# Sample stage of a hybrid decoder step: one DMA per cache page, TensorE in written order with rows of the output projection as filler, output weights loaded ahead of the pages

## The chip, the cores and the metric

The kernel runs on one NeuronCore of a Trainium2 chip. The metric is the device time of one execution in microseconds (us). Before the change three runs took 1098.09, 1099.56 and 1103.59 us; their median, 1099.56 us, is the number to beat.

## What is computed

The reference is one step of a layer with three groups of heads that all read the same projection of the normalised input: an NSA group (compressed, selected and window attention), an RWKV-7 group and a memory group. Their outputs are gated, concatenated and multiplied by one output projection `w_out`. There is a prompt of 1024 rows and a batch of 8 samples with one new row each, whose past of 1024 rows lies in 8 cache pages that a page table names. The part that matters here is what is done for the samples, and the output projection:

```python
def nsa_decode_seq(q, pt_row, rows4_new, rows_w_new, win_buf, gates, pool, ...):
    past = pool[pt_row].reshape(-1, 4, NSA_KV_HEADS, HEAD_DIM)       # 8 pages of 128 rows
    rows4 = jnp.concatenate([past, rows4_new], axis=0)
    ck, cv, cend, ksb, vsb, ov = nsa_context(rows4, ...)             # compressed keys and values
    o_c, o_s = cmp_sel_attend(q, qpos, ck, cv, cend, ksb, vsb, ov)   # compressed and selected attention
    ...

def mixer_out(o_nsa, z_nsa, o_rw, z_rw, o_mem, z_mem, w_out):
    cat = jnp.concatenate([o_nsa.reshape(b, t, NSA_W) * jax.nn.silu(z_nsa),
                           o_rw * jax.nn.silu(z_rw), o_mem.reshape(b, t, MEM_W) * jax.nn.silu(z_mem)], axis=-1)
    return cat @ w_out
```

## The kernel before

The program has three phases. `phase1` projects the input, `phase2` does the attention of the prompt with the small work of the samples between its parts, and `phase3` does the NSA attention of the samples and the output projection of everything. The change is in phase 3, and in how memory is shared out between phases 2 and 3.

A page of the cache is laid out in memory as 128 rows of 512 numbers: 256 that the compression reads (`x`) and 256 with the selected keys and values (`kv`). `pages` loads the 8 pages of one sample: SyncE (SP) reads the page's number from the table into a register and issues two DMAs of 128 KB, one for each half. `compress` then multiplies the `x` half of a sample with the weights of the compression, 16 matmuls a sample into the tiles `p_hid`, with two short chains of ScalarE (ACT) and VectorE (DVE) work behind them. After four samples `nsa_four` takes the group on: compressed keys and values (`p_co`), a norm and rotation on DVE, transposes (`p_ckT`), scores (`p_cs`), a softmax, the choice of blocks (`p_cT`, `p_imp`), the long softmax over 1025 columns (`s_sel`), transposes of it (`p_PT`), the sum over values (`p_os`) and the last transpose (`p_oT`). Each of these steps waits for the one before it, and most of them go from TensorE (PE) to DVE or ACT and back. The scores of the selected keys (`p_ss`) are made ahead of it. Sample 0's pages are loaded in phase 2.

The prompt's output projection is cut in two halves of 512 columns. `wo_half` loads 8 pieces of `w_out` (`wor`, 256 KB each, through a pool `wst` of 4 buffers) and splits each into a rounded part `woh` (ACT) and a remainder `wol` (DVE). `out_rows` does one block of 128 rows: 24 matmuls into `p_out`, after `split_cat` has split the block's input into `chi` (ACT) and `clo` (DVE); GpSimd (POOL) loads the residual `xres` and stores the sum. There are 8 blocks a half, and `out_proj_sample` does the 8 sample rows with the weights of both halves at the end.

The order in phase 3 is set by the scheduler of the tile framework, by what is ready and by the order in which the code is written: the pages of both groups are written first, half 1 (`W1`) is written ahead of the second `nsa_four`, half 0 (`W0`) behind it. A helper `InOrder` pins TensorE's instructions to the written order; phase 2 uses it with a clock that adds up the matmuls' sizes, so that generators of work can be interleaved by that clock. Phase 3 before the change uses TensorE directly.

Pools of one phase stand where pools of the phase before stood, and a tile of the new phase waits until the tiles under it have been used for the last time. `small2` and `wk` come first in phase 2, `small3`, `wk3`, `wst` and `wop` in phase 3.

Of the kernel before, what the change touches and what calls it, by code (L numbers as in the profile page):

```python
# [21 lines left out]
NS = 8  # L22
# [4 lines left out]
KB = 2  # L27
# [9 lines left out]
RATE = {i: (0.8, 0.8, 1, 1) if i > 3 else (1.5, 1.5, 1.5, 0) for i in range(8)}  # L37
START = (1.0, 0.0, 0.7, 0.0)
# [74 lines left out]
class Step:  # L113
# [846 lines left out]
    def compress(self, xt, n, hid):  # L960

        nc = self.nc
        V, A, PE = nc.vector, nc.scalar, nc.tensor
        V.memset(hid[:, :, 63:64], 0.0)
        for e in range(2):
            ps = self.pM.tile([128, n, 64], F32, name="p_hid", tag="m")
            for m in range(8):
                self.last_hid = PE.matmul(ps[:], self.w1s[e][:, m].rearrange("p a b -> p (a b)"), xt(e, m), start=(m == 0), stop=(m == 7))  # L968
            hs = self.wk.tile([64, n, 63], F32, name="c_hs", tag="c_hs")
            A.activation(hs[:], ps[64:, :, 1:], AF.Copy)  # L970
            V.tensor_tensor(hs[:], hs[:], ps[:64, :, :63], op=OP.add)
            th = self.wk.tile([64, n, 63], F32, name="c_th", tag="c_th")
# [198 lines left out]
    def q_stack(self, i):  # L1171
# [3 lines left out]
        q = self.kt.tile([128, 12, 64], F32, name="q7") if first else self.wk.tile([128, 12, 64], F32, name="q", tag="q", bufs=2)  # L1175
        nc.sync.dma_start(q[:].rearrange("p h d -> p (h d)"), self.q_d[i * 128:(i + 1) * 128, :])
        qs = self.qs[i] = (self.kt if i % 2 else self.wk).tile([128, 12, 128], F32R, name="qs", tag="qs")
        for b in (0, 1, 2):
            pool, tag, nb = (self.kt, "kd4", KB) if first else (self.wk, "qhl", 2)
# [9 lines left out]
    def load_z(self, i):  # L1189
        cat = self.cat[i] = self.slot(i, [128, 8, 128], F32, f"cat{i}")  # L1190
        y = self.y_rw[i] = self.wk.tile([128, 256], F32, name="y_rw", bufs=2)
# [3 lines left out]
    def attn_cmp(self, i):  # L1195
# [5 lines left out]
        sc = self.wk.tile([128, 4, 128], F32, name="sc", tag="sc")  # L1201
# [10 lines left out]
        pcq = self.wk.tile([128, 8, 64], F32, name="pcq", tag="pcq")  # L1212
# [131 lines left out]
    def attn_mem(self, i):  # L1344
# [5 lines left out]
        for c in range(2):  # L1350
            nm = self.small.tile([128, 2], F32, name="nm_m")
            sm = self.small.tile([128, 2], F32, name="sm_m")
            pm = self.wk.tile([128, 2, 256], F32, name="pmem", tag="pmem", bufs=2)
# [84 lines left out]
    def phase2(self):  # L1438
        tc, nc, I, O = self.tc, self.nc, self.I, self.O
        with ExitStack() as ctx:  # L1440
            P = lambda name, bufs, **k: ctx.enter_context(tc.tile_pool(name=name, bufs=bufs, reuse_waits="tile", **k))
            self.small = P("small2", 2)
            self.wk = P("wk", 1)
# [127 lines left out]
    def sample_setup(self):  # L1571
# [9 lines left out]
        qmb = self.qmb = self.wk.tile([128, 2, NS, 32], F32, name="qmb")  # L1581
# [7 lines left out]
        x, sq, xr = (self.wk.tile([128, 8, NS], F32, name=f"s_x{k}") for k in range(3))  # L1589
# [12 lines left out]
        tab = self.wk.tile([128, 7, NS], F32, name="s_tab")  # L1602
# [65 lines left out]
    def four_keys(self, name, n):  # L1668
# [6 lines left out]
        return KT + [self.wk.tile([128, 512], F32, name=name, tag="sk", bufs=3)[:] for _ in range(2)]  # L1675

    def four_pT(self, p, n):
# [5 lines left out]
        pT = self.wk.tile([128, 4, 128], F32, name="s_pT", tag="s_pT")  # L1683
# [3 lines left out]
    def sample_mem(self):  # L1687
# [15 lines left out]
        def rest(a, p):  # L1703
# [8 lines left out]
            o = self.wk.tile([128, 256], F32, name="m_o", tag="s_p")  # L1712
# [14 lines left out]
        for a in range(2):  # L1727
# [10 lines left out]
            p = self.wk.tile([128, 256], F32, name="m_p", tag="s_p")  # L1738
# [4 lines left out]
    def sample_win(self):  # L1743
# [24 lines left out]
        def rest(a, p):  # L1768
# [8 lines left out]
            o = self.wk.tile([128, 128], F32, name="w_o", tag="s_p")  # L1777
# [9 lines left out]
        for a in range(2):  # L1787
# [8 lines left out]
            p = self.wk.tile([128, 512], F32, name="w_p", tag="s_p")  # L1796
# [4 lines left out]
    def pages(self, s, x, kv):  # L1801

        nc = self.nc
        for j in range(8):
            with self.tc.issue_after(self.last_page.ins):
                n = nc.sync.value_load(self.ptab[0:1, 8 * s + j:8 * s + j + 1], min_val=0, max_val=self.I["c_pool"].shape[0] - 1)  # L1806
            page = self.I["c_pool"][bass.ds(n, 1)].rearrange("o p c -> (o p) c")
            nc.sync.dma_start(x[:, j], page[:, 0:256])  # L1808
            self.last_page = nc.sync.dma_start(kv[:, j], page[:, 256:512])  # L1809

    def nsa_ahead(self):
# [8 lines left out]
        self.pg = [self.arena(k, "pg")[:].rearrange("p (n c) -> p n c", n=8) for k in range(2)]  # L1820
# [3 lines left out]
    def sample_nsa(self):  # L1824
# [3 lines left out]
        with ExitStack() as ctx:  # L1828
# [15 lines left out]
            with P("snsx") as xp:  # L1844

                def place(name):
                    if name in ("a0", "a1"):
                        t = self.arena(int(name[1]), "pg")[:]
                    else:
                        t = fresh.pop(name, None) or xp.tile([128, 2048], F32, name="pg", tag=name)  # L1850
                        t = t[:]
                    return t.rearrange("p (n c) -> p n c", n=8)

                fresh = {}
                for name in ("x0", "x1", "v2", "v3", "v1", "v4", "v5"):
                    fresh[name] = xp.tile([128, 2048], F32, name="pg", tag=name)
                X = [None, "x0", "x1", "a0", "x0", "x1", "a0", "x0"]
                K = [None, "v1", "v2", "v3", "v4", "v5", "v1", "a1"]
                for a in range(2):
                    VS = []  # L1860
                    hid = dp.tile([128, 4, 2, 64], F32, name="shid")
                    for s in range(4 * a, 4 * a + 4):
                        if s:
                            x, kv = place(X[s]), place(K[s])
                            self.pages(s, x, kv)
                        else:
                            x, kv = self.pg
                        VS.append(kv)
                        xm = x.rearrange("p n (e g m c) -> p e m g n c", e=2, g=2, m=8)
# [4 lines left out]
                    with tc.issue_after(self.last_hid.ins):  # L1874
                        for h in range(2):
                            for k in range(4):
                                PE.matmul(pS[h][32 * k:32 * k + 32], self.qb[:, 4 * a + k, :], VS[k][:, 4 * h:4 * h + 4, 0:128],
                                          start=True, stop=True)
                    if a:
                        W1 = self.wo_half(self.wop, 1)  # L1880
                        self.out_proj_prompt(1, W1)
                    self.nsa_four(a, hid, pS, VS, vn, dp)
            W0 = self.wo_half(ctx.enter_context(P("wop2")), 0)
            self.out_proj_prompt(0, W0)
            self.out_proj_sample((W0, W1))

    def nsa_four(self, a, hid, pS, VS, vn, dp):
# [13 lines left out]
        o = self.norm_rope(ck[:].rearrange("p s d -> p (s d)")[:, None, :], 3, 1, 4, 9)  # L1901
        pk = self.pT.tile([128, 4, 128], F32, name="p_ckT", tag="t")
# [3 lines left out]
        V.tensor_copy(kt[:], pk[:64])  # L1906
        pc = self.pM.tile([128, 128], F32, name="p_cs", tag="m")
# [13 lines left out]
        V.tensor_copy(im[:], pi[:])  # L1921
        pi2 = self.pM.tile([128, 16], F32, name="p_imp2", tag="m")
# [13 lines left out]
        V.tensor_scalar(sc[:], sc[:], self.gr[:, a, 0:1], None, op0=OP.mult)  # L1936
        srcs = [sl[:, j * 128:(j + 1) * 128] for j in range(8)] + [sc[:]]
        for j0, j1 in ((0, 4), (4, 8), (8, 9)):
# [3 lines left out]
            (A.activation if j0 == 4 else V.tensor_copy)(PTs[:, j0:j1], pp[:, :j1 - j0], *((AF.Copy,) if j0 == 4 else ()))  # L1942
        po = self.pT.tile([128, 128], F32, name="p_os", tag="t")
# [5 lines left out]
        V.scalar_tensor_tensor(oS[:], vn[:, a, :], sl[:, 1024:1025], po[:], op0=OP.mult, op1=OP.add)  # L1949
        pt = self.pM.tile([128, 4, 32], F32, name="p_oT", tag="m")  # L1950
# [329 lines left out]
```

## Time and profile before

| | |
|---|---|
| median of 3 runs | 1099.56 us (1098.09 to 1103.59) |
| profiled execution | 1105.1 us, its span 1103.3 us |
| mean granted TensorE clock | 0.948 |
| TensorE busy | 982.6 us, 89% |
| DVE, ACT, POOL busy | 686.0, 482.6, 37.2 us |
| chain that ended last | PE 64%, DVE 16%, ACT 7%, SP queue 6%, issue 4%, DMA 3% |

Times in the views are microseconds from the first instruction. The page cuts the span into 40 slices of 27.6 us; the digits are tenths of busy time, and the row PEclk gives the clock that TensorE was granted, in tenths of full speed. In the groups the number after the bar is the idle time of the engine before these instructions and what ended it. An fp32 matmul stands as two matmuls in the trace: the 16 of a sample's compression are x32 there.

### The profile page before, as it was taken

Reading aid. Unit: us, or ns where it says so; the run is one execution under the profiler, and the core shown is the slowest. Engines: PE = TensorE matmul, PEld = TensorE weight load, DVE = VectorE, ACT = ScalarE, POOL = GpSimd, SP = SyncE. Lnnn points to the kernel's source line nnn. Section 1 sums busy time; section 2 is a strip of 40 time slices with the busy share of each in tenths; the row PEclk is TensorE's granted clock in tenths of the full one; section 3 lists DMA queues with packets and bytes.
Section 4 is the critical chain, followed back from the end, with each engine's and each line's share of the span. In section 5 each row is a group of like instructions: output and inputs, shape, how many; then the busy total and the mean of one; then the engine's idle time right before and its main releaser. Section 6 shows DMA issues by size and latency. Waiting matters only on the chain.

```text
span 1103.3 us, 27205 instructions
## 1 busy us (share of the span) xinstructions
PE 982.6 (89%) x11167; PEld 817.5 (74%) x11167; DVE 686.0 (62%) x2001; ACT 482.6 (44%) x1063; POOL 37.2 (3%) x84
## 2 busy tenths in 40 slices
PE   6999999999999999999879999999997944699398
PEld 5998788668887787878657777878786743578276
DVE  7667389446935982634476886878898713523642
ACT  6553234323522433234367777767876510322120
POOL 1000000000000000000000001000000000001011
PEclk9999899999999999999979999999999966699699
DMA  7323113213221173261461225121002555552031
GB/s 257 96 59 87 42 44 108 64 41 86 77 61 31 44 182 78 77 178 43 146 202 59 90 90 168 26 58 35 12 28 78 124 160 152 183 161 96 21 112 52
DMA packets 133988, 102.27 MB, mean 93 GB/s; under 512 B 35105, under 2 KB 121640, under 8 KB 133736
## 3 DMA queue, kind: packets, MB, share of 16 engines
q1 hardware_dynamic: 129544, 90.93, 28.8%
q0 software_dynamic: 2560, 8.39, 2.3%
q8 instruction: 88, 1.44, 0.6%
q10 hardware_dynamic: 1760, 1.21, 0.4%
q14 instruction: 36, 0.29, 0.1%
HBM read 81.91 MB, written 22.78 MB: 95 GB/s over the span
## 4 chain that ended last, share of the span: by engine, by line
PE 64%; DVE 16%; ACT 7%; SPq 6%; issue 4%; DMA 3%; POOL 0%; DVEq 0%; ACTq 0%; POOLq 0%
PE p_pr L85 16%; PE p_pr L267 7%; PE p_out L2133 7%; PE p_s L85 5%; PE p_o L85 4%; PE p_pT L85 4%; PE p_it L85 3%; SPq L1806 2%; SPq L1809 2%; SPq L1808 2%; PE p_hid L968 1%; PE p_z L85 1%; ACT p L1292 1%; DVE nm L1291 1%; PE p_iy L85 1%
## 5 line engine op out<-in xcount | busy, mean ns | idle before, releaser
L85 PE MATMUL p_pr<-h,whi 128*128 128x512 f32 (+5 forms) x928 | 233.8, 343 | 0.0
L85 PEld LDWEIGHTS p_pr<-h,whi 128*128 128x128 f32 (+1 forms) x928 | 147.2, 185 | 18.0 <-issue 3.0
L85 PE MATMUL p_pr<-h,wlo 128*128 128x512 f32 (+5 forms) x464 | 153.1, 330 | 0.0
L85 PEld LDWEIGHTS p_pr<-h,wlo 128*128 128x128 f32 (+1 forms) x464 | 85.9, 185 | 9.6
L267 PE MATMUL p_pr<-h,whi 128*128 128x256 f32 (+2 forms) x416 | 88.5, 308 | 0.3 <-ACT whi L254 0.3
L85 PE MATMUL p_pT<-ident,p 128*128 128x128 f32 x528 | 73.7, 285 | 5.8 <-ACT pt L1250 3.3
L85 PE MATMUL p_s<-kh,qs 128*128 128x512 f32 (+3 forms) x191 | 72.2, 386 | 3.2 <-ACT p L1292 3.2
L85 PEld LDWEIGHTS p_pT<-ident,p 128*128 128x128 f32 x528 | 58.7, 144 | 17.6 <-issue 7.3
L85 PE MATMUL p_o<-pt,vs 128*64 128x128 f32 x1056 | 70.3, 283 | 1.0 <-DVE c_r L1226 0.6
L267 PEld LDWEIGHTS p_pr<-h,whi 128*128 128x128 f32 x416 | 67.4, 192 | 3.5 <-ACT whi L254 0.7
L255 DVE TENSOR_TENSOR wlo<-wraw,whi 128x1024 fp32r<-128x1024 f32 (+1 forms) x35 | 41.8, 1198 | 44.1 <-ACT whi L254 43.5
L1291 DVE TENSOR_REDUCE nm<-p_s 128x1 f32<-128x640 f32 (+3 forms) x64 | 57.6, 918 | 18.0 <-PE p_s L85 17.9
L1292 ACT ACTIVATE p<-p_s,nm 128x640 f32<-128x640 f32 (+3 forms) x64 | 55.7, 874 | 24.9 <-DVE nm L1291 24.1
L85 PEld LDWEIGHTS p_o<-pt,vs 128*64 128x64 f32 x1056 | 59.2, 140 | 6.7 <-issue 2.7
L267 PE MATMUL p_pr<-h,wlo 128*128 128x256 f32 (+2 forms) x208 | 63.3, 306 | 0.0
L85 PE MATMUL p_s<-kl,qs 128*128 128x512 f32 (+3 forms) x192 | 62.8, 343 | 0.0
L968 PE MATMUL p_hid<-pg,w1a 128*128 128x128 f32 x256 | 38.5, 323 | 25.4 <-DMA pg<-in_c_pool_dram 22.6
L254 ACT ACTIVATE whi<-wraw 128x1024 fp32r<-128x1024 f32 (+1 forms) x35 | 36.3, 1037 | 50.2 <-PE p_pr L85 36.3
L1252 DVE COPY pt<-p_pT 128x512 f32<-128x512 f32 (+1 forms) x72 | 48.1, 671 | 15.7 <-PE p_pT L85 15.3
L968 PEld LDWEIGHTS p_hid<-pg,w1a 128*128 128x128 f32 x256 | 37.4, 237 | 26.8 <-issue 26.5
L2133 PE MATMUL p_out<-woh,chi 128*128 128x512 f32 x128 | 51.0, 399 | 2.1 <-ACT woh L2122 2.1
L2133 PE MATMUL p_out<-wol,chi 128*128 128x512 f32 x128 | 50.6, 398 | 0.1
(533 smaller groups left out, 2011.5 us busy)
## 6 DMA issues: line engine op xcount, KB each, us to landing
wraw<-in_w_in_dram SPq DMA_DIRECT2D x34, 512.0 KB
pg<-in_c_pool_dram SPq DMA_DIRECT2D x128, 128.0 KB
x<-in_x_prompt_dram SPq DMA_DIRECT2D x8, 512.0 KB
z_d<-zt SPq DMA_DIRECT2D x16, 256.0 KB
cat<-z_d SPq DMA_DIRECT2D x8, 512.0 KB
xres<-in_x_prompt_dram POOLq DMA_DIRECT2D x16, 256.0 KB, 3.1
wor<-in_w_out_dram SPq DMA_DIRECT2D x16, 256.0 KB
out_dram<-xres POOLq DMA_DIRECT2D x16, 256.0 KB, 2.5
```

The lines of the kernel that those rows point to most:

```text
L85: self.last = getattr(self.engine, op)(*a, **k)
L254: nc.scalar.activation(hi[:, :, :n], raw[:, :, :n], AF.Copy)
L255: nc.vector.tensor_tensor(lo[:, :, :n], raw[:, :, :n], hi[:, :, :n].bitcast(F32), op=OP.subtract)
L267: self.last_mm = self.pe.matmul(ps[:m, :b - a], w[:, k, :m], h[k][:, a:b], start=(k == 0 and i == 0), stop=(k == 7 and i == 2))
L968: self.last_hid = PE.matmul(ps[:], self.w1s[e][:, m].rearrange("p a b -> p (a b)"), xt(e, m), start=(m == 0), stop=(m == 7))
L1252: nc.vector.tensor_copy(pt[:, :n], ps[:, :n])
L1291: V.tensor_reduce(nm[:, h, b:b + 1], ps[:, c0:n1], axis=AX.X, op=OP.max, negate=True)
L1292: A.activation(Ps[h, b][:, :n1 - c0], ps[:, c0:n1], AF.Exp, bias=nm[:, h, b:b + 1], accum_out=sm[:, h, b:b + 1])
L1806: n = nc.sync.value_load(self.ptab[0:1, 8 * s + j:8 * s + j + 1], min_val=0, max_val=self.I["c_pool"].shape[0] - 1)
L1808: nc.sync.dma_start(x[:, j], page[:, 0:256])
L1809: self.last_page = nc.sync.dma_start(kv[:, j], page[:, 256:512])
L2133: self.te.matmul(po[:rows], c[:, k, :rows], w[:], start=(k == 0 and j == 0), stop=(k == 7 and j == 2))
```

## The change

It does six things.

1. `pages` issues one DMA of 256 KB for a page of samples 1 to 6, with both halves as its target (two chunks of one tile `big` of 7 chunks); samples 0 and 7 keep two DMAs. The bounds of the page's number are no longer given, so no check of it is made.
2. The first pages are held behind the last load of `W1` (`self.last_page = self.last_wor`).
3. `W1` is loaded and split at the start of phase 3. `wst` has 3 buffers and not 4. `W0` goes into the same tiles as `W1` once half 1 is done, and `W1` is loaded a second time at the end for the samples: 24 loads of `wor` in all, where there were 16.
4. TensorE is in written order through all of phase 3 (`InOrder`). `sample_nsa` is now a generator that says at each step how many us of other work should come before its next step (`WAIT` behind a sample's compression, 0.8 to 7.5 in `nsa_four`), and `phase3` fills these with the output projection, three matmuls at a time. Behind the first `nsa_four` it fills until half 1 is done.
5. `c_hs` and `c_th` of the compression have two buffers each.
6. Tiles of phase 2 are moved from `wk` into a pool `we` ahead of it, so that the first pools of phase 3 lie over them.

The core of the diff (the pool's name in 16 places of phase 2 is left out):

```diff
+WAIT = (10.0, 5.0, 5.0, 0.0, 0.0, 0.0, 0.0, 0.0)
...
-    def pages(self, s, x, kv):
+    def pages(self, s, x, kv=None):
...
-                n = nc.sync.value_load(self.ptab[0:1, 8 * s + j:8 * s + j + 1], min_val=0, max_val=self.I["c_pool"].shape[0] - 1)
+                n = nc.sync.value_load(self.ptab[0:1, 8 * s + j:8 * s + j + 1])
             page = self.I["c_pool"][bass.ds(n, 1)].rearrange("o p c -> (o p) c")
-            nc.sync.dma_start(x[:, j], page[:, 0:256])
-            self.last_page = nc.sync.dma_start(kv[:, j], page[:, 256:512])
+            c = slice(256 * j, 256 * j + 256)
+            if kv is None:
+                self.last_page = nc.sync.dma_start(x[:, :, c], page.rearrange("p (a c) -> p a c", a=2))
+            else:
+                nc.sync.dma_start(x[:, c], page[:, 0:256])
+                self.last_page = nc.sync.dma_start(kv[:, c], page[:, 256:512])
...
+                big = xp.tile([128, 7, 2048], F32, name="pg")
+                at = {1: (0, 2), 2: (1, 3), 3: (0, 4), 4: (1, 5), 5: (0, 6), 6: (1, 2)}
...
+                self.last_page = self.last_wor
                 for a in range(2):
...
                     for s in range(4 * a, 4 * a + 4):
+                        x, kv = load(s)
...
+                        yield WAIT[s]
...
-                    if a:
-                        W1 = self.wo_half(self.wop, 1)
-                        self.out_proj_prompt(1, W1)
-                    self.nsa_four(a, hid, pS, VS, vn, dp)
-            W0 = self.wo_half(ctx.enter_context(P("wop2")), 0)
-            self.out_proj_prompt(0, W0)
-            self.out_proj_sample((W0, W1))
+                    yield from self.nsa_four(a, hid, pS, VS, vn, dp)
+                    if a == 0:
+                        yield None
+            W1 = self.wo_half(ctx.enter_context(P("wop2")), 1)
+            yield 1e6
+            self.out_proj_sample((self.W0, W1))
...
+    def out_prompt(self):
+        yield from self.out_proj_prompt(1, self.W1)
+        self.W0 = self.wo_half(self.wop, 0)
+        self.half = 1
+        yield from self.out_proj_prompt(0, self.W0)
...
-            self.wst = P("wst", 4)
+            self.wst = P("wst", 3)
...
-            self.sample_nsa()
+            self.W1, self.half = self.wo_half(self.wop, 1), 0
+            self.te = InOrder(tc, tc.nc.tensor, None)
+            fill, main = self.out_prompt(), self.sample_nsa()
+            while True:
+                with tc.high_priority(offset=FIRST):
+                    us = next(main, -1)
+                if us == -1:
+                    break
+                end = self.te.clock + (us or 0)
+                while self.te.clock < end or us is None and not self.half:
+                    if next(fill, 0) == 0:
+                        break
```

What this does to the engines' rows is shown at three places. In these rows `wor` is a piece of `w_out` on its way in, `pt` the page table, `v_new` the new values of the samples, and `ISA` an instruction on registers. First SP where phase 3 begins; before:

```order
L1834 DMA v_new<-out_dram 32x2x128 x4
L1808 ISA
L1808 DMA pg<-in_c_pool_dram 128x256
L1809 ISA
L1809 DMA pg<-in_c_pool_dram 128x256
L1806 TENSOR_LOAD pt
L1806 ISA x2
```

and after:

```order
L2130 DMA wor<-in_w_out_dram 128x512 x3
L1840 DMA v_new<-out_dram 32x2x128 x4
L2130 DMA wor<-in_w_out_dram 128x512 x5
L1808 TENSOR_LOAD pt
L1812 ISA
L1812 DMA pg<-in_c_pool_dram 128x2x256
```

The eight loads of `W1` now stand ahead of the first page, and a page is three instructions and not six. Second SP between the pages of samples 5 and 6, after the change (before, nine loads of `wor` stand between two pages of sample 5, and seven behind the last page):

```order
L1812 DMA pg<-in_c_pool_dram 128x2x256
L2130 DMA wor<-in_w_out_dram 128x512 x11
L1808 TENSOR_LOAD pt
L1812 ISA
L1812 DMA pg<-in_c_pool_dram 128x2x256
```

The eight loads of `W0` and the first three of the second `W1` stand ahead of the pages of samples 6 and 7. Third TensorE, from the first group's products to the second's; before:

```order
L968 MATMUL p_hid<-pg,w1a 128x128 x64
L1877 MATMUL p_ss<-pg,qb 32x512 x8
L1894 MATMUL p_co<-w2d,shid 128x128 x4
L1904 MATMUL p_ckT<-ident,nr_o 64x128 x4
L1909 MATMUL p_cs<-ckt,q_7882 32x128 x4
L1914 MATMUL p_cT<-ident,s_c 128x128
```

and after, from the end of the first group on:

```order
L86 MATMUL p_os<-s_cv,PTs 32x128 x4
L86 MATMUL p_out<-woh_13025,chi 128x512
L86 MATMUL p_out<-wol_13022,chi 128x512
L86 MATMUL p_out<-woh_13025,clo 128x512
L86 MATMUL p_out<-woh_13031,chi 128x512
L86 MATMUL p_out<-wol_13028,chi 128x512
L86 MATMUL p_out<-woh_13031,clo 128x512
L86 MATMUL p_oT<-ident,oS 128x128
L86 MATMUL p_hid<-pg,w1a 128x128 x64
L86 MATMUL p_ss<-pg,qb 32x512 x8
L86 MATMUL p_co<-w2d,shid 128x128 x4
```

Before, samples 0 to 3 stand in one piece with no product of the projection between them. After, 45, 24 and 24 matmuls of `p_out` stand behind samples 0, 1 and 2, and 111 between `p_co` and `p_oT` of each group; between the compressions of samples 4, 5, 6 and 7 there are none, and behind the second `p_oT` 69 are left. TensorE's row of phase 2 is the same before and after.

More of the change, by code (lines that the diff above doesn't have):

```diff
@@ L1174, in q_stack @@
         first = i == 7
-        q = self.kt.tile([128, 12, 64], F32, name="q7") if first else self.wk.tile([128, 12, 64], F32, name="q", tag="q", bufs=2)
+        q = self.kt.tile([128, 12, 64], F32, name="q7") if first else self.we.tile([128, 12, 64], F32, name="q", tag="q", bufs=2)
         nc.sync.dma_start(q[:].rearrange("p h d -> p (h d)"), self.q_d[i * 128:(i + 1) * 128, :])
@@ L1190, in load_z @@
         cat = self.cat[i] = self.slot(i, [128, 8, 128], F32, f"cat{i}")
-        y = self.y_rw[i] = self.wk.tile([128, 256], F32, name="y_rw", bufs=2)
+        y = self.y_rw[i] = self.we.tile([128, 256], F32, name="y_rw", bufs=2)
         self.nc.sync.dma_start(y[:], self.y_d[i * 128:(i + 1) * 128, :])
@@ L1200, in attn_cmp @@
         gate = self.gates[:, i, :].rearrange("p (h b) -> p h b", b=3)
-        sc = self.wk.tile([128, 4, 128], F32, name="sc", tag="sc")
+        sc = self.we.tile([128, 4, 128], F32, name="sc", tag="sc")
         for g in range(2):
@@ L1587, in sample_setup @@
         rows = self.sample_tables()
-        x, sq, xr = (self.wk.tile([128, 8, NS], F32, name=f"s_x{k}") for k in range(3))
+        x, sq, xr = (self.we.tile([128, 8, NS], F32, name=f"s_x{k}") for k in range(3))
         o = c.tile([128, 8, NS], F32, name="s_o")
@@ L1674, in four_keys @@
             KT = [two[:, 0], two[:, 1]]
-        return KT + [self.wk.tile([128, 512], F32, name=name, tag="sk", bufs=3)[:] for _ in range(2)]
+        return KT + [self.we.tile([128, 512], F32, name=name, tag="sk", bufs=3)[:] for _ in range(2)]
     def four_pT(self, p, n):
@@ L1819, in nsa_ahead @@
         self.load_w1([w1[:, e * 1024:e * 1024 + 1024].rearrange("p (j s h) -> p j s h", j=8, s=2) for e in range(2)])
-        self.pg = [self.arena(k, "pg")[:].rearrange("p (n c) -> p n c", n=8) for k in range(2)]
+        self.pg = [self.arena(k, "pg")[:] for k in range(2)]
         self.pages(0, *self.pg)
@@ L1844, in sample_nsa, with load @@
             with P("snsx") as xp:
-                def place(name):
-                    if name in ("a0", "a1"):
-                        t = self.arena(int(name[1]), "pg")[:]
-                    else:
[L1850 to L1858, printed above, removed]
+                big = xp.tile([128, 7, 2048], F32, name="pg")
+                at = {1: (0, 2), 2: (1, 3), 3: (0, 4), 4: (1, 5), 5: (0, 6), 6: (1, 2)}
+                def load(s):
+                    if s in at:
+                        i, j = at[s]
+                        self.pages(s, big[:, i:j + 1:j - i])
+                        x, kv = big[:, i], big[:, j]
+                    else:
+                        x, kv = self.pg if s == 0 else [self.arena(k, "pg")[:] for k in range(2)]
+                        if s:
+                            self.pages(s, x, kv)
+                    return x, kv.rearrange("p (n c) -> p n c", n=8)
+                self.last_page = self.last_wor
                 for a in range(2):
```

60 lines of the change are left out of this document (33 added, 27 removed).

## Prediction

> **What bounds the kernel now.** I read the page's slices first, to see where TensorE (PE) is not busy, then the same stretch by windows, then PE's timeline there, then SP's own instructions.
>
> ```profile
> PE   6999999999999999999879999999997944699398
> PEclk9999899999999999999979999999999966699699
> ```
>
> PE is full nearly everywhere; the holes are slices 33 to 35 and 38, in the sample stage, and the granted clock falls there too.
>
> ```profile
> 878.00:925.00 47.00, 24.36 (x150) 22.35 (x150) 9.23 (x33) 5.39 (x16) 1.67 (x3) 0.71 0.54 166
> 950.00:982.50 32.50, 29.38 (x230) 25.12 (x228) 14.47 (x38) 10.39 (x22) 2.17 (x4) 0.92 0.63 191
> ...
> 1021.00:1051.40 30.40, 13.10 (x115) 8.83 (x115) 17.68 (x58) 5.78 (x12) 0.78 (x2) 0.66 0.14 46
> ...
> 878.00:1103.30 225.30, 160.35 (x918) 128.68 (x918) 86.55 (x217) 41.48 (x77) 18.22 (x34) 0.82 0.39 120
> ```
>
> The columns are the length, the busy time of PE, PEld, DVE, ACT and POOL, the clock, the DMA engines' share and GB/s. The whole phase 3 is the last row: 225 us with PE busy for 160 at a clock of 0.82, so some 65 us are idle.
>
> ```profile
> 874.36 0.38 PE L85 MATMUL p_yT<-ident,y_rw 128*128 128x128 f32 x2
> ...
> 877.64 0.31 PE L1841 MATMUL p_new<-s_o,qb 128*32 128x1 f32 x16
> 878.03 3.81 PE L968 MATMUL p_hid<-pg,w1a 128*128 128x128 f32 x32
> 889.41 5.99 PE L968 MATMUL p_hid<-pg,w1a 128*128 128x128 f32 x32 [7.57 <-DMA pg<-in_c_pool_dram]
> 903.07 5.99 PE L968 MATMUL p_hid<-pg,w1a 128*128 128x128 f32 x32 [7.67 <-DMA pg<-in_c_pool_dram]
> 916.42 6.13 PE L968 MATMUL p_hid<-pg,w1a 128*128 128x128 f32 x32 [7.37 <-DMA pg<-in_c_pool_dram]
> ```
>
> Phase 3 starts at 877.64 with `p_new`. Samples 1 to 3 each wait 7.4 to 7.7 us for their pages. The pages wait for SP, which the chain of waits shows at work without a pause:
>
> ```profile
> 882.42 0.05 SPq L1809
> ...
> 882.57 0.33 SPq L1809
> ...
> 882.94 0.28 SPq L1806
> ...
> 883.28 0.15 SPq L1806
> ...
> 883.55 0.05 SPq L1808
> ...
> 883.70 0.34 SPq L1808
> ...
> 884.09 0.05 SPq L1809
> ...
> 884.23 0.33 SPq L1809
> ```
>
> That is one page: from one second DMA (882.57) to the next (884.23, 0.53 behind the first at 883.70) are 1.66 us, 13.3 for a sample; the engines that move the data are busy for a share of 0.54. After the pages, PE waits inside `nsa_four`:
>
> ```profile
> PE p_ckT L1904 <- DVE nr_o L359: 13.1, 2, 7.1
> PE p_PT L1941 <- DVE s_sel L1666: 12.5, 2, 6.2
> ```
>
> **The change, step by step.** I sum phase 3 from `p_new` to the end: 1103.3 - 877.64 = 225.7 us now. PE's row of phase 2 does not move, so phase 2 is costed at nothing.
>
> *One DMA a page.* From the rows above: the table read to the next instruction takes 0.34 (882.94 to 883.28), the check with its arithmetic 0.27 (to 883.55) falls away, the address takes 0.15 (to 883.70), a DMA 0.39 (to 884.09), and the second DMA with its address falls away. So 0.34 + 0.15 + 0.39 = 0.88 us a page. What one DMA with two pieces a row costs to issue isn't in the trace for this form; the nearest rows are
>
> ```profile
> L1808 SPq DMA_DIRECT2D pg<-in_c_pool_dram x64: 337/338/373, 839.1 to 980.2; - x64
> L1021 SPq DMA_DIRECT2D wraw<-in_w_mem_kv_dram x4: 378/384/619, 480.6 to 525.3; - x4
> L915 SPq DMA_DIRECT2D w1a<-in_cmp_w_dram x4: 522/1146/1914, 854.4 to 858.2; - x4
> ```
>
> (ns, least, median, most). `w_mem_kv` also goes in as two pieces a row, of 2 KB, at 384 ns; `w1a` has eight pieces of 256 B and takes 1146. The bounds of a page are thus 0.88 and 0.88 + 0.81 = 1.69; I take 0.9, by the row that is like it. Samples with two DMAs a page (7) need 0.88 + 0.53 = 1.41.
>
> *W1 ahead.* Eight loads pass three buffers ahead of the first page. By
>
> ```profile
> 1046.91 3.81 DMA wor<-in_w_out_dram
> ...
> 1050.74 0.64 ACT woh L2122
> ```
>
> a load takes 3.8 us and its split 0.64 on ACT and 0.69 on DVE (row of `wol` below), some 5.5 a round with the issue, three rounds. The first waits for a tile under it that is read by `p_yT` (at 874.36, above), so the eighth weight is there at about 891, 14 us into phase 3, and the pages start at about +10 (before: -3). PE has the 3.8 us of sample 0 and then the first filler row, 24 matmuls (5.5 us), which needs each weight as it comes: it ends at 14.5 and not 9.6, a **stall of 5** (0 if the loads come earlier, 10 if a round takes as long again as its splits). The pages of samples 1 to 5, 40 x 0.9 = 36 us, then hide behind PE's 93 filler matmuls and the first group.
>
> *PE's work.* By
>
> ```profile
> 956.28 7.15 PE p_hid L968 x64
> ...
> 987.90 1.85 PE p_ss L1877 x16
> ...
> 1027.68 1.07 PE p_ckT L1904 x4
> ...
> 1040.62 1.99 PE p_PT L1941 x8
> ...
> 1043.27 2.64 PE p_os L1947 x72
> ...
> 1051.42 40.67 PE p_out L2133 x176
> 1092.09 7.40 PE p_out L2171 x32
> 1099.49 0.02 issue
> ```
>
> two samples' compression takes 7.15 at full clock, so eight 28.6; `p_ss` 2 x 1.85 = 3.7; the projection 384 x 40.67/176 = 88.7; the small products of `nsa_four` 1.07 + 1.99 + 2.64 and some 3.5 for the six shorter ones, 9.2 a group at the clock of 0.66 that the window from 1021 shows, so about 7 at a full one, 14 for two; the samples' projection 7.4; `p_new` 0.4. Together 142.8. The second load of `W1` (8 x 0.48 on SP, 1.3 on ACT and DVE each) lies beside the last 69 filler matmuls (16 us); were these gone it would cost some 10.
>
> *Written order inside `nsa_four`.* The fillers (111 matmuls, 25.6 us a group) now cover the waits. But ACT and DVE also do the fillers' share:
>
> ```profile
> L2144 DVE TENSOR_TENSOR clo<-cat,chi 128x1024 fp32r<-128x1024 f32 x16 | 19.5, 1224 | 2.6 <-ACT chi L2143 2.6
> L2136 DVE TENSOR_TENSOR xres<-xres,p_out 128x512 f32<-128x512 f32 x16 | 11.0, 688 | 48.3 <-PE p_out L2133 48.3
> L2123 DVE SCALAR_TENSOR_TENSOR wol<-wor,woh 128x512 fp32r<-128x512 f32 x16 | 10.9, 688 | 6.7 <-ACT woh L2122 6.6
> ```
>
> 1.9 us on DVE a block, in program order between the steps of the softmax. Each of the two long waits meets one or two such blocks, so PE stands for about 3 us at `p_ckT` and at `p_PT`; in the first group the splits of `W0` stand in the same rows, since they wait for the last reads of `W1`. I take **7.5** for the first group, **4** for the second (bounds 0 and 15 for both).
>
> *Pages of samples 6 and 7.* Their targets are read by sample 4's compression and the first `p_os`, and they stand on SP behind 11 loads of `wor`. So they start about 3.6 us after `p_oT`, and need 8 x 0.9 + 8 x 1.41 = 18.5 and a landing, by
>
> ```profile
> 978.12 2.58 DMA pg<-in_c_pool_dram
> ```
>
> of 2.6: 24.7 us after `p_oT`, while PE has three compressions to do, 10.7. A **stall of 14**, and sample 7 then runs at the low clock: 6.0 and not 3.6 (the rows at 889.41 and 878.03), 2.4 more. No filler stands there, so this is the largest stall that the change makes.
>
> The Trainium skill, page "TensorE: Matmul & The Clock Gate" (section "What's actually happening"), says that the array runs at half its clock after about 3.4 us of idling, and back at full after 3.4 us of work. By that rule alone sample 7 would cost 7.2 us, and the sum would be 1.2 higher; the row of 5.99 us decides.
>
> *End and pauses.* From 1099.49 to 1103.3 are 3.8, as now. SP pauses now and then:
>
> ```profile
> 880.11 1.13 SPq L1809 DMA_DIRECT2D pg<-in_c_pool_dram  x1
> ```
>
> once in some 40 us; one on the path, 1.1.
>
> Sum: 142.8 + 5 + 7.5 + 14 + 2.4 + 4 + 3.8 + 1.1 = 180.6 us in place of 225.7, a gain of 45. The profiled execution took 1105.1 us, 5.5 over the median; I take the gain off the median: 1099.6 - 45 = **1054.5 us**.
>
> **Rivals.** *The transfers become the bound.* Let a page take p on the DMA side or on SP. When that is longer than PE's work beside it, phase 3 is: 9.5 to the first page, 24 p, a landing, then compression, `p_ss`, the first group with its fillers and stalls (25.6 + 7 + 7), sample 4, 16 p, a landing, sample 7 (6), `p_ss`, the second group (7 + 4), 180 fillers (41.6), 7.4 and 3.8: about 135 + 40 p. At full share the stretch from 950 would move 191/0.63 = 303 GB/s (an estimate from its row); less 512 KB of residual in and out a block of 5.5 us, 95 GB/s, 208 are left, which is p = 1.26 and 185.4 us: 1059. If p stays at 1.66, 201.4 us: 1075. For it speaks that the share is 0.54 at 1.66 us a page already; against it that it is not more.
>
> The Trainium skill, page "DMA: Bandwidth & Descriptors" (section "Issuing engines are not separate DMA queues"), holds the time to issue a DMA to be usually small beside the DMA itself. By that p would stay and this rival's upper end would come true; SP without a pause at a share of 0.54 speaks against it here.
>
> *The chain through DVE and ACT is late.* With 4 us at each of the seven waits of a group, 2 x 28 in place of 11.5: 1099, no change; with 2 us, 1071. For it: strict order on all three engines; against: fillers of 7 to 7.5 us stand at the long waits, which are 6.2 to 7.1 now.
>
> *The loads ahead don't come ahead.* If the tiles under `W1` come free only at 877.6, the stall is 8 and not 5: 1057.5; within the likeliest.
>
> *Better.* If only the stall for samples 6 and 7 is left: 142.8 + 16.4 + 3.8 = 163: 1037.
>
> *Slower.* One mechanism: the issue of the merged DMA. From 135 + 40 p the gain is gone at p = 2.27, an issue of 1.7 us. `w1a` reached 1.9 at most; its median is 1.15, with pieces a quarter the size. At p = 2.5 it is 1109.
>
> **Chances.** Likeliest (1046 to 1062) 0.62; transfers 0.15 (1059 to 1075); late chain 0.08 (to 1080), with no change a third of it; better 0.09; slower 0.04; 0.02 for other ways to no change. The range leaves out the better half of "better", the end of the late chain and the slower ones, together under 2 in 10: 1043 to 1074. Half a per cent, 5.5 us, is about what the three runs tell from no change. Faster 0.92, same 0.04, slower 0.04.
>
> **What the profile would show.** SP's page at about 0.9 us with one DMA; samples 1 to 3 without a wait for pages; `p_out` between them; a clock near 0.95 in slices 32 to 34; one hole of 14 us ahead of sample 7, and short waits at `p_ckT` and `p_PT`. Wrong: a DMA share near 0.9 with pages still waited for, a DMA on SP of 0.8 us or more, or PE waits at each step of `nsa_four`.

## The result, and the profile after

The changed kernel takes 1054.53 us, the median of 4 runs (1052.12 to 1054.81); the kernel before, run beside it, 1098.82 (1097.91 to 1103.59). The ratio is 0.958, with a 95% interval from 0.955 to 0.962. The forecast was 1054.5. The profiled execution after took 1054.74 us, with a span of 1053.0.

The page of the changed kernel again has 40 slices, now of 26.3 us. The holes in slices 33 to 35 and in 38 are gone, and with them the clock of 0.6; what is left is shallower, in 37 and 38, with a clock of 0.7 in the latter.

```profile
PE   5999999989999999999987999999999888996898
PEclk9999999999999999999998999999999999999799
```

By windows, the whole of phase 3 and two stretches in it (length, busy time of PE, PEld, DVE, ACT and POOL, clock, DMA share, GB/s):

```profile
876.06:1053.00 176.94, 151.77 (x936) 121.06 (x934) 89.50 (x221) 46.54 (x87) 17.61 (x33) 0.94 0.51 164
...
898.06:932.67 34.61, 33.10 (x198) 28.02 (x198) 16.45 (x54) 8.37 (x17) 3.79 (x7) 0.96 0.89 282
...
962.50:990.20 27.70, 16.75 (x97) 16.33 (x96) 5.04 (x18) 4.05 (x12) 0.00 (x0) 0.69 0.50 152
```

Phase 3 takes 176.9 us in place of 225.7, with the clock at 0.94 and not 0.82. The stretch of samples 1 to 3 and the head of the first group is now full on PE, and the data engines stand at 0.89 there. The stretch from 962.5, that of samples 6 and 7, is the one place left where PE idles for long. PE's timeline has each sample:

```profile
876.06 0.19 PE L83 MATMUL p_new<-s_o,qb 128*32 128x1 f32 x1
...
876.45 3.81 PE L86 MATMUL p_hid<-pg,w1a 128*128 128x128 f32 x32
...
898.06 5.19 PE L86 MATMUL p_hid<-pg,w1a 128*128 128x128 f32 x32 [2.62 <-issue]
...
908.59 3.73 PE L86 MATMUL p_hid<-pg,w1a 128*128 128x128 f32 x32
917.64 3.73 PE L86 MATMUL p_hid<-pg,w1a 128*128 128x128 f32 x32
...
958.35 0.33 PE L86 MATMUL p_oT<-ident,oS 128*128 128x128 f32 x1 [0.24 <-DVE oS L1958]
958.78 7.38 PE L86 MATMUL p_hid<-pg,w1a 128*128 128x128 f32 x64
973.97 6.43 PE L86 MATMUL p_hid<-pg,w1a 128*128 128x128 f32 x32 [7.82 <-DMA pg<-in_c_pool_dram]
983.54 6.75 PE L86 MATMUL p_hid<-pg,w1a 128*128 128x128 f32 x32 [3.13 <-DMA pg<-in_c_pool_dram]
```

Sample 1 waits 2.6 us; samples 2 and 3, which waited 7.7 and 7.4, don't wait; samples 6 and 7 wait 7.8 and 3.1 and run at the low clock. The list of PE's waits from 876 on (total, times, longest) has nothing else of this size. The 13.1 us at `p_ckT` of before are 2.3; the 12.5 at `p_PT` for `s_sel` are 1.2, with 1.1 for `PTs` beside them:

```profile
PE p_hid L86 <- DMA pg<-in_c_pool_dram: 10.9, 2, 7.8
PE p_hid L86 <- issue: 2.6, 1, 2.6
PE p_ckT L86 <- DVE nr_o L360: 2.3, 2, 1.5
PE p_out L86 <- ACT woh L2132: 1.7, 2, 1.3
PE p_PT L86 <- DVE s_sel L1668: 1.2, 2, 0.6
PE p_PT L86 <- DVE PTs L1950: 1.1, 2, 0.8
PE p_out L86 <- DVE wol L2133: 0.9, 4, 0.2
```

SP's part of the chain of waits shows one page, from one DMA at 888.54 to the next, and further down the landing of sample 1's seventh page:

```profile
888.54 0.54 SPq L1812
...
889.13 0.27 SPq L1808
...
889.44 0.04 SPq L1812
...
889.58 0.54 SPq L1812
...
892.70 4.02 DMA pg<-in_c_pool_dram
```

A page is 1.04 us: 0.27 for the table, 0.54 for the one DMA, 0.23 for the address and between them. Still one instruction behind the other. Sample 1's eighth page is issued at 894.15, and PE begins with the sample at 898.06, 3.9 us later. That this is what its 2.6 us waited for is read from these times: the profile names no releaser there (`issue`).

### The profile page after: what moved, and what is told of

Its sections match the earlier page's. It is cut to its first block, busy times and chain, and to the rows that moved or that the text cites. A ratio compares the mean times of both kernels' runs of the same rounds, so it can differ in the third digit from the quotient of the medians.

```text
span 1053.0 us, 26959 instructions
## 1 busy us (share of the span) xinstructions
PE 969.5 (92%) x11167; PEld 805.1 (76%) x11167; DVE 688.7 (65%) x2009; ACT 485.1 (46%) x1071; POOL 36.8 (3%) x84
## 4 chain that ended last, share of the span: by engine, by line
PE 67%; DVE 16%; ACT 6%; DMA 4%; issue 3%; SPq 3%; POOL 0%; DVEq 0%; ACTq 0%; POOLq 0%
PE p_pr L86 18%; PE p_pr L268 7%; PE p_out L86 6%; PE p_s L86 5%; PE p_o L86 4%; PE p_pT L86 4%; PE p_it L86 3%; PE p_hid L86 2%; PE p_z L86 1%; DVE nm L1292 1%; ACT p L1293 1%; DMA wor<-in_w_out_dram 1%; PE p_iy L86 1%; DVE pt L1253 1%; DVE wlo L256 1%
## 5 line engine op out<-in xcount | busy, mean ns | idle before, releaser
L1293 ACT ACTIVATE p<-p_s,nm 128x640 f32<-128x640 f32 (+3 forms) x64 | 55.7, 873 | 26.0 <-DVE nm L1292 25.2
L1253 DVE COPY pt<-p_pT 128x512 f32<-128x512 f32 (+1 forms) x72 | 48.0, 670 | 13.1 <-PE p_pT L86 12.7
L86 PE MATMUL p_out<-woh,clo 128*128 128x512 f32 x128 | 50.1, 391 | 0.0
L86 PE MATMUL p_hid<-pg,w1a 128*128 128x128 f32 x256 | 37.0, 315 | 13.7 <-DMA pg<-in_c_pool_dram 10.9
```

Source lines behind the costliest of these rows:

```text
L86: self.last = getattr(self.engine, op)(*a, **k)
L1253: nc.vector.tensor_copy(pt[:, :n], ps[:, :n])
L1293: A.activation(Ps[h, b][:, :n1 - c0], ps[:, c0:n1], AF.Exp, bias=nm[:, h, b:b + 1], accum_out=sm[:, h, b:b + 1])
```

## The experiments

All times are medians; the kernel before took 1099.6 to 1100.8 in the comparisons below. In some of them the length of phase 3 in the profiled execution is told as well (from `p_new` to the end of the span), since the end of phase 2 lies anywhere from 871.9 to 877.6 us in these executions, and a median of 4 to 8 runs bears that scatter. The length of phase 3 is that of one execution.

**The order without the pages' part.** The changed kernel with the pages as they were:

```diff
-                        self.pages(s, big[:, i:j + 1:j - i])
                         x, kv = big[:, i], big[:, j]
+                        self.pages(s, x, kv)
...
-                n = nc.sync.value_load(self.ptab[0:1, 8 * s + j:8 * s + j + 1])
+                n = nc.sync.value_load(self.ptab[0:1, 8 * s + j:8 * s + j + 1], min_val=0, max_val=self.I["c_pool"].shape[0] - 1)
```

> The changed kernel with the pages as before: two DMAs and the bounds check for each page, 1.66 us by the rows of before; the written order and the loads ahead stay. Theory (SP's instructions set the pages, and the pages set samples 1 to 3): sample 3's pages land 24 x 0.56 = 13 us later, of which some 12 reach the first group, samples 6 and 7 cost 6 more, the loads of W0 come later behind the pages for another 0 to 6: 1072 to 1080 us. Rival (rows of the projection hide the pages whatever they take): at most 1060.

Measured: 1076.1 us (1074.1 to 1078.7), ratio 0.977 [0.973, 0.981]. PE's waits for pages are back, although all rows of the projection stand between the samples as in the changed kernel:

```profile
PE p_hid L86 <- DMA pg<-in_c_pool_dram: 24.4, 3, 10.9
PE p_PT L86 <- DVE s_sel L1668: 6.1, 2, 5.5
PE p_hid L86 <- issue: 4.8, 2, 3.5
```

That is 29.2 us for five samples, against 13.5. The 5.5 us at `p_PT` come of the pages too: the weights of `W0` are loaded behind them, ACT's first split of `W0` waits 4.8 us for its weight, and the softmax stands behind that split. All of the change but the pages' part is worth 24.7 us; rows of the projection don't hide pages of 1.66 us. What the written order, the second buffers of the compression and the moved tiles are worth by themselves, no run tells.

**The pages' part without the order.** The kernel before, with one DMA a page, no bounds check, and the seven tiles in one that this needs:

```diff
-                n = nc.sync.value_load(self.ptab[0:1, 8 * s + j:8 * s + j + 1], min_val=0, max_val=self.I["c_pool"].shape[0] - 1)
+                n = nc.sync.value_load(self.ptab[0:1, 8 * s + j:8 * s + j + 1])
...
-            nc.sync.dma_start(x[:, j], page[:, 0:256])
-            self.last_page = nc.sync.dma_start(kv[:, j], page[:, 256:512])
+                self.last_page = nc.sync.dma_start(x[:, :, c], page.rearrange("p (a c) -> p a c", a=2))
```

> The kernel before with one thing of the change: one DMA a page and no bounds check, in the changed kernel's places (seven tiles in one). Theory: a page takes about 1.05 us in place of 1.66, samples 1 to 3 wait some 4.8 us less each, 14 together, and a few us more at samples 6 and 7: 1078 to 1086 us. Rival (the pages were not what samples 1 to 3 waited for, the order brings it all): 1094 to 1100.

Measured: 1079.7 us (1078.1 to 1081.7), ratio 0.981 [0.978, 0.985]. SP issues 37 pages in a row at 1.06 us each. Of PE's long waits on DVE those at `p_ckT` and at the second `p_PT` stay as long as they were:

```profile
875.50 39.10 SPq L1810 DMA_DIRECT2D pg<-in_c_pool_dram  x37
...
PE p_ckT L1906 <- DVE nr_o L359: 13.1, 2, 7.1
PE p_hid L968 <- DMA pg<-in_c_pool_dram: 8.2, 1, 8.2
PE p_PT L1943 <- DVE s_sel L1666: 6.3, 1, 6.3
PE p_hid L968 <- issue: 5.2, 1, 5.2
```

At the first `p_PT` the scheduler now puts 12 products of the projection, whose weights are loaded from 914.7 on and not from 944.4, and 3.4 us of waiting are left there. So the pages' part alone is worth 21.1 us, a part of them in that wait. 21.1 and 24.7 are 45.8; both together brought 44.3, so the two parts nearly add up.

**Two DMAs, without the check.** The part of the first experiment's diff above its `...` alone.

> The changed kernel with two DMAs a page for all samples, still without the bounds check. Theory (SP issues without a pause, so the page is what SP's instructions take): sample 7's period of 1.36 us for all, 0.33 more a page than 1.03; sample 3 lands 8 us later, sample 6 2.6: 1061 to 1068 us. Rival (in the stretch of samples 1 to 5 the engines that move the data are the bound, at a share of 0.89): the period stays at 1.1 and the time at 1054 to 1057.

Measured: 1063.7 us (1061.4 to 1065.8), ratio 0.967 [0.963, 0.970]. Its SP has 1.36 us a page, from 900.33 to 901.70 and on (columns as in the chain above):

```profile
900.33 0.33 SPq L1814
...
900.86 0.33 SPq L1815
...
901.70 0.33 SPq L1814
```

So the data engines, though at 0.89 in the changed kernel, did not set its period. With the first experiment the pages' part divides: the bounds check is worth about 12 us (1076.1 to 1063.7), the second DMA about 9 (1063.7 to 1054.5). The Trainium skill, page "DMA: Bandwidth & Descriptors" (section "Issuing engines are not separate DMA queues"), holds the time to initiate a DMA to be usually small beside the DMA itself. Here it isn't: a page of 256 KB is followed by the next after 1.66, 1.36 or 1.04 us, by what SP has to execute, and the kernel's time goes with it.

**No rows between.** The changed kernel with the first half of the projection whole behind the first group, the second behind the second:

```diff
-                end = self.te.clock + (us or 0)
-                while self.te.clock < end or us is None and not self.half:
+                while us == 1e6 or us is None and not self.half:
```

> The changed kernel without rows of the projection between samples 0 to 3 and inside the groups: the first half of the projection stands whole behind the first group, the second half behind the second. Theory (the rows cover idle time): samples 1 to 3 then wait for their pages and the 20 us of rows there come back at the end, 18 us net; in each group 25.6 us of rows covered about 19 of waiting: 1095 to 1112 us, as slow as the kernel before or slower. Rival (the gain is the pages', the rows only fill what would be hidden anyway): 1060 to 1075.

Measured: 1107.9 us (1106.5 to 1114.3), ratio 1.0065 [1.0036, 1.0095]: by less than 1% slower than the kernel before, with the faster pages in it. The waits are those of before, and one of 17 us for sample 1, whose pages stand behind W1's eight loads:

```profile
PE p_hid L86 <- DMA pg<-in_c_pool_dram: 29.6, 3, 17.3
PE p_PT L86 <- DVE s_sel L1668: 12.5, 2, 6.3
PE p_ckT L86 <- DVE nr_o L360: 12.0, 2, 6.0
```

The rows are worth 53 us to this kernel, whose TensorE order is fixed; before, the scheduler put products of the projection between samples 4 to 7. Without the rows the loads ahead delay sample 1's pages and win nothing that the run shows.

**Loads not ahead.** The changed kernel without the line that holds the pages back:

```diff
-                self.last_page = self.last_wor
```

> The changed kernel without the one line that puts the pages behind the loads of W1: on SP the 16 pages of samples 1 and 2 then stand between W1's third and fourth load. Theory (the loads ahead are worth what PE's first row of the projection would wait for them): that row gets its fourth weight behind 16.5 us of pages and its eighth three rounds later, so sample 1 starts at about 906 and not 898, while samples 2 and 3 wait less than now; p_ss starts 4 to 7 us later: 1057 to 1063 us. Rival (the order of the loads doesn't matter, SP has the same work): 1052 to 1057.

Measured: 1065.5 us (1062.4 to 1067.7), ratio 0.970 [0.966, 0.974]; phase 3 is 187.7 us. SP has 16 pages, then the loads, and PE stands for them:

```profile
875.39 16.25 SPq L1812 DMA_DIRECT2D pg<-in_c_pool_dram  x16
891.74 11.91 SPq L2129 DMA_DIRECT2D wor<-in_w_out_dram  x8
...
896.43 0.80 PE L86 MATMUL p_out<-woh,chi 128*128 128x512 f32 x1 [17.22 <-ACT woh L2131]
```

The mechanism is as expected, the price was low by 2.5 at least: sample 1 starts 35.8 us after `p_new` (872.94) and not 30, and samples 2 and 3 could win nothing back, since they don't wait in the changed kernel either. The loads ahead are worth 11 us.

**Rows beside the pages of samples 6 and 7.**

```diff
-WAIT = (10.0, 5.0, 5.0, 0.0, 0.0, 0.0, 0.0, 0.0)
+WAIT = (10.0, 5.0, 5.0, 0.0, 0.0, 9.0, 4.0, 0.0)
```

> The changed kernel with 9 us of rows of the projection behind sample 5 and 4 us behind sample 6, taken from the 16 us that stand at the end. Theory (the waits for the pages of samples 6 and 7, 7.8 and 3.1 us, and their compression at the low clock, 6.4 and 6.8 us for 3.7, lie on the path): sample 7 starts when its pages land, as now, but runs 3 us shorter, 13 us of rows are out of the end, and of the second load of W1, whose cover they were, some 4 us come to light: 1040 to 1046 us. Rival (the rows at the end are needed there to cover W1, 10 us): 1050 us or more.

Measured: 1040.8 us (1038.3 to 1042.1), ratio 0.946 [0.943, 0.950]; phase 3 is 162.2 us. Sample 6 no longer waits, and sample 7 runs at the full clock:

```profile
984.38 3.81 PE L86 MATMUL p_hid<-pg,w1a 128*128 128x128 f32 x32 [2.44 <-DMA pg<-in_c_pool_dram]
```

Phase 3 is 14.7 us shorter: of the hole's 16.6 us (10.9 of waits, 5.7 of low clock) all but sample 7's 2.4 are gone, so it was on the path. No wait for W1's second load appears in PE's list behind it: 3 us of rows at the end were enough cover.

**Samples 6 and 7 exchanged.**

```diff
-                at = {1: (0, 2), 2: (1, 3), 3: (0, 4), 4: (1, 5), 5: (0, 6), 6: (1, 2)}
+                at = {1: (0, 2), 2: (1, 3), 3: (0, 4), 4: (1, 5), 5: (0, 6), 7: (1, 2)}
```

> The changed kernel with the places of samples 6 and 7 exchanged, the waits as they are: sample 6 goes to the two tiles of sample 0, which are free when the first group's p_os ends (956.5) and not when sample 4's compression ends (962.5), and keeps two DMAs a page; sample 7 gets the merged ones. Theory (the tiles set when these pages start, SP how long they take): SP begins at about 958.5, sample 7's pages land at 958.5 + 10.9 + 8.2 + 2.6 = 980.2 and not 983.5: 1049 to 1053 us. Rival (the loads of the weights ahead of them hold SP): no change, 1054 to 1056.

Measured: 1049.7 us (1047.4 to 1055.4), ratio 0.956 [0.951, 0.960]; phase 3 is 171.7 us, 5 less.

```profile
957.31 7.38 PE L86 MATMUL p_hid<-pg,w1a 128*128 128x128 f32 x64
968.20 5.44 PE L86 MATMUL p_hid<-pg,w1a 128*128 128x128 f32 x32 [3.50 <-DMA pg<-in_c_pool_dram]
978.72 5.79 PE L86 MATMUL p_hid<-pg,w1a 128*128 128x128 f32 x32 [5.08 <-DMA wor<-in_w_out_dram]
```

Sample 7 starts 21.4 us behind the start of sample 4's compression and not 24.8, and all but half a page of these pages are issued from 955.72 on, 1.6 us ahead of that start. In the changed kernel SP had put out its last load of `wor` by 958.4 and the first page went out at 962.62, when sample 4's compression was done: there the tiles, and not SP, set when these pages begin. (The profile puts sample 7's wait down to a load of `wor`; SP issues that load right behind sample 7's last page, and the sample reads pages alone.) By its interval the time can't be told apart from the changed kernel's; what tells them apart is the place of sample 7 in one execution of each.

**Both, and more rows behind sample 0.** The exchange, with

```diff
-WAIT = (10.0, 5.0, 5.0, 0.0, 0.0, 0.0, 0.0, 0.0)
+WAIT = (12.0, 5.0, 5.0, 0.0, 0.0, 7.0, 3.0, 0.0)
```

> Both of these, with 12 us of rows behind sample 0 (10 before), 7 behind sample 5 and 3 behind sample 6. Theory: sample 7 starts at about 980 and runs at the full clock, which is 6 us to the end of its compression; 10 us less of rows at the end; the wait of 2.6 us for sample 1's pages filled, with 1.5 of the low clock: 1034 to 1041 us. Rival (cover of W1 lost at the end): 1043 to 1048.

Measured: 1036.2 us (1032.6 to 1037.6), ratio 0.941 [0.938, 0.945]; phase 3 is 158.6 us. This is the version that beats both: 18 us off the changed kernel. Of the waits for pages 1.9 are left at sample 1 and 0.6 at sample 7.

**Pages on two queues.** Every other page of samples 1 to 7 is read and issued by POOL:

```diff
+            q = nc.gpsimd if s and j % 2 else nc.sync
...
-                n = nc.sync.value_load(
+                n = q.value_load(
...
-                self.last_page = nc.sync.dma_start(x[:, :, c], page.rearrange("p (a c) -> p a c", a=2))
+                p = q.dma_start(x[:, :, c], page.rearrange("p (a c) -> p a c", a=2))
```

> The changed kernel with every other page of samples 1 to 7 read and issued by POOL, the rest by SP. Theory (SP's instructions set the page's period, and the engines that move the data have room): sample 1 isn't waited for, 4 us, and the pages of samples 6 and 7 take about 10 us less, which takes away that much of waiting and 2 to 3 of the low clock: 1036 to 1043 us. Rival (at a share of 0.89 and 282 GB/s in the stretch of samples 1 to 5 the data are the bound, and POOL's own DMAs wait for the rows of the projection): the pages land no earlier, 1050 to 1058 us.

Measured: 1046.7 us (1045.7 to 1046.8), ratio 0.952 [0.949, 0.955]. Neither theory: 8 us won, not 11 to 18. Sample 1 indeed doesn't wait. But POOL puts its eight pages of samples 1 and 2 out while W1 is still loading, and W1's last weights now wait for the data engines: the last five of its loads land 5.3 to 6.6 us after their issue, and not 2.6 to 4.9 (PE's timeline, then the window around it):

```profile
889.80 0.80 PE L86 MATMUL p_out<-woh,chi 128*128 128x512 f32 x1 [3.31 <-ACT woh L2135]
...
885.00:893.00 8.00, 4.69 (x11) 2.80 (x10) 1.51 (x3) 1.49 (x3) 0.00 (x0) 0.50 1.03 350
...
971.25 3.96 PE L86 MATMUL p_hid<-pg,w1a 128*128 128x128 f32 x17 [6.16 <-DMA pg<-in_c_pool_dram]
```

At 350 GB/s and a share of 1.03 the data engines are full in this window: one queue at 255 GB/s (256 KB in 1.03 us) stays under that. From `p_new` to the end of sample 3 nothing is won (873.27 to 920.5, 47.2 us; 45.3 without this edit); the gain is at samples 6 and 7, which wait 6.2 and not 10.9, and of which sample 7 runs at the full clock. That two issuing engines share one set of data engines and only save sequencer time is what the same section of the Trainium skill says, and this run agrees, with the 350 GB/s.

**Still more rows behind sample 0.** The version of 1036.2 with 14.5 in place of 12.

> The exchange of samples 6 and 7 with rows of the projection behind samples 0, 5 and 6, as before, but 14.5 us behind sample 0 in place of 12. Theory (every wait left over is filled by rows from the end until the second load of W1 loses its cover): the wait for sample 1's pages, 1.9 us, and 1.7 of low clock go, and W1's last weight, which comes 1 us before it is needed now, is waited for about 1.5 us: 1032 to 1036 us, 2 below 1036.2. Rival (the cover at the end is worth what it was put at in the prediction, 10 us for 16 of rows): 1037 or more.

Measured: 1036.0 us (1033.6 to 1037.4, 5 runs), ratio 0.942 [0.939, 0.946]; phase 3 is 158.75 us. No change.

```profile
873.75:1032.50 158.75, 145.45 (x936) 115.06 (x934) 90.26 (x221) 47.84 (x87) 17.58 (x33) 0.99 0.58 183
...
PE p_PT L86 <- DVE s_sel L1668: 2.9, 1, 2.9
...
PE p_hid L86 <- DMA pg<-in_c_pool_dram: 1.2, 1, 1.2
...
PE p_out L86 <- DVE c_s L2176: 1.1, 1, 1.1
```

Sample 1 doesn't wait any more. But the first `p_PT` has 2.9 us in one wait (0.8 and 1.8 in the version of 1036.2), and the clock falls there, to 0.50 from 949.7 to 953.1; 1.2 us stand at sample 7 (0.6 there) and 1.1 at the samples' projection (none there). That the first of these comes from the splits of W0 is a reading of their place: on ACT two of them, each waiting some 0.5 us for its weight, stand ahead of the softmax, which starts 1.7 us behind its maximum (0.5 in the changed kernel). No run tried it by itself. The wait for W1 that was expected did not come. PE now works for 145.5 of 158.75 us at a clock of 0.99; of the 13.3 that are left 3.9 are the end, so what is left to win by order is below 10 us.

## Why the prediction was right, point by point

That the number was right to the tenth is luck. The sum for phase 3 was 3.7 us too long, with errors of both signs in its terms, and taking the gain off the median and not off the profiled execution made up for it. Against the timeline after:

| term | forecast | measured |
|---|---|---|
| PE's work at full clock | 142.8 | 151.8 busy less 7.2 of low clock = 144.6 |
| start: W1, sample 1 | 5 | 2.5 idle for weights + 2.6 for pages + 1.5 of low clock = 6.6 |
| first group | 7.5 | 1.5 + 0.6 + 0.8 + 0.2 = 3.1 |
| samples 6 and 7, waits | 14 | 7.8 + 3.1 = 10.9 |
| samples 6 and 7, low clock | 2.4 | 2.7 + 3.0 = 5.7 |
| second group | 4 | 1.8 |
| end | 3.8 | 3.9 |
| SP pause | 1.1 | 0.4 ahead of sample 1's eighth page, within its 2.6 |
| sum | 180.6 | 176.6; by the window 176.9 |

- *One DMA a page.* The step whose size failed: 0.9 us was forecast, 1.04 is measured, 1.10 as a mean over 40 (44.0 us on SP from 886.36). Table and address came as forecast (0.32 and 0.14, with the gaps); the DMA with two pieces a row takes 0.54 to issue, 0.58 with its gap, and not the 0.39 taken by the row of `w_mem_kv`. The trace of before did hold a row of the very form, two pieces of 1 KB a row, from a fixed address, and the prediction passed it over:

```profile
L1700 SPq DMA_DIRECT2D mxv<-in_cache_mem_dram x8: 545/582/612, 542.5 to 598.6; - x8
```

With its 0.55 to 0.58 a page comes to 1.04 to 1.07. The 1.04 lay inside the bounds (0.88 to 1.69) and cost little, because samples 2 and 3 had slack. Sample 1 had none: its eighth page was issued 7.8 us behind its first (6.3 at 0.9 a page), and PE started 3.9 us behind that, where 2.6 was taken for the landing. Its wait of 2.6 was not forecast.

- *W1 ahead.* The pages began 10.3 us after `p_new`, as forecast (+10), and the first row of 24 products ended 14.6 us after it, as forecast (14.5). So the stall of 5 came; the table has 2.5 of it as idle time, and the rest stands in PE's busy time, where many of these products start 0.5 to 0.7 us apart and not 0.23. The work itself is thus nearer 142 than 144.6. The fall back to no hold costs 11 us.
- *Written order.* The direction was right; 11.5 us at the groups were too many by 6.6. One or two blocks of the projection's splits in each long wait cost far less than 3 us there, as long as the weights of `W0` are in time: with the old pages they weren't, and 5.5 us stood at one `p_PT`.
- *Samples 6 and 7.* The best step: start of the pages 4.3 us after `p_oT` (3.6 forecast), sample 7's arrival 25.2 after it (24.7). But it was drawn as one hole ahead of sample 7. The larger wait stands ahead of sample 6, and so two samples run cold, not one, and a cold sample 6 hides part of sample 7's wait; together 16.6 for 16.4. Their 6.4 and 6.8 us are longer than the row of 5.99, which the sum went by. The 7.2 us that the prediction took from the rule of the Trainium skill ("TensorE: Matmul & The Clock Gate", "What's actually happening") doesn't follow from it: full speed back after some 3.4 us of work makes 3.4 for the first 1.7 us of the sample's 3.6 and 1.9 for the rest, an estimate of 5.3. Here the clock stayed at 0.50 for 5.5 us of sample 6's work (to 979.47) and for 6.2 us of sample 7's (to 989.71).
- *Cover at the end.* "Some 10" us for the second load of W1, were its rows gone, was wrong: 14.5 us of rows went elsewhere in the last kernel, and no wait for W1 appeared.
- *Rivals.* Transfers as the bound, by 135 + 40 p: at p = 1.66 it gave 1075, and the kernel with the old pages took 1076.1; by phase 3, 201.4 and 201.9. At 1.36 it gives 189.4, and that kernel took 182.9 (from 877.6 to 1060.4): its groups wait for 4.7 us, and not for the 11 that are in the 135. At 1.04 it gives 176.6, and 176.9 were measured, but not for its reason: samples 2 and 3 don't wait for pages there. So the pages as the bound hold for the old page, and p fell because SP's instructions did. *Late chain* and *slower* found nothing: 1.8 to 3.1 us a group, an issue of 0.54 and not 1.7. *Better* did not come: beside the hole 6.6 us were left at the start and 4.9 in the groups.
- *The base.* The profiled pair differs by 50.4 us (1105.1 to 1054.7), the medians by 44.3. Phase 3 lost 48.7 and not the 45.1 of the forecast; taking the gain off the median assumed that the 5.5 us by which the profiled execution of before was slow do not belong to phase 3. Where they lie stays open: phase 3 began at 877.6 there, at the late end of the range told above.

## What to carry to other kernels

Where transfers are issued one by one from a table, count the issuing engine's instructions for one of them, table read and bounds check and all, and put that period beside what the data engines can do; here it was the period of samples 1 to 3, with the data engines at a share of 0.54. When an in-order engine is given filler, place it by when data arrive, and look for the stretch where none stands: here 13 us of it, moved from the end to one hole, brought 14 more. A second issuing queue helped here until the data engines were full, and then it delayed the weights that were loading beside it.

## What was not expected of the hardware

TensorE's clock fell to half at pauses of 1.9 to 2.6 us, but not at all of them. Sample 1 after 2.62 us ran at 0.50; in the version of 1036.2, after 1.89, it ran at 0.62 in the mean of its first 3.3 us. In the kernel with rows beside the pages of samples 6 and 7, sample 1 lost the clock after 2.36 us and sample 7 kept it after 2.44 (windows of the changed kernel, of the version of 1036.2, and two of the latter):

```profile
898.06:900.00 1.94, 1.94 (x9) 1.94 (x10) 0.00 (x0) 0.00 (x0) 0.00 (x0) 0.50 0.96 318
...
899.66:903.00 3.34, 3.34 (x19) 3.34 (x20) 0.00 (x0) 0.27 (x1) 0.00 (x0) 0.62 0.87 301
...
897.14:900.00 2.86, 2.86 (x15) 2.86 (x16) 0.00 (x0) 0.00 (x0) 0.00 (x0) 0.56 0.95 322
984.38:987.00 2.62, 2.62 (x23) 2.62 (x24) 0.25 (x1) 0.27 (x1) 0.00 (x0) 1.00 0.03 6
```

The traces' clock records show where the difference lies. The clock changes on a grid: in the changed kernel the five stretches from 897.55 on, at half and at full speed by turns, last 3.41, 68.27, 10.24, 3.41 and 6.83 us, all multiples of 3.41. The pause of 2.36 us lay whole in one piece of such a grid (894.09 to 897.50, PE busy for 1.05 us of it), and the clock fell at that piece's end. The pause of 2.44 lay across two (979.41 to 986.23, PE busy for 2.53 and 1.85 us), and the clock stayed. The piece at whose end the version of 1036.2 lost the clock (900.47) had PE busy for 1.52 us. So where a pause lies counts, and not its length alone. How much work in a piece keeps the clock stays open: in the kernel before a piece with 1.51 us kept it (880.33 to 883.74).

The Trainium skill, page "TensorE: Matmul & The Clock Gate" (section "What's actually happening"), asks for an idle window of about 3.4 us before the clock drops, and calls the window free-running. The grid agrees with the second. A piece with 1.52 us of work in it that costs the clock doesn't fit the first, if idle means without work.

And an issue of one DMA on SP took 0.33 us for one piece a row, 0.54 for two pieces of 1 KB (pages, from an address in a register; `mxv` from a fixed one 0.55 to 0.61), 0.38 for two of 2 KB (`w_mem_kv`), 0.37 for eight of 512 B (`w_in`): it follows neither the bytes nor the pieces alone.
